# Mixture-of-experts kernel: gates read in eleven pieces at first, 40 instead of 32 first halves computed ahead

## The chip, the cores and the metric
One core of a Trainium2 chip runs the whole program. The metric is the device time of one execution in microseconds. Lower is better.

## What is computed
The reference runs two blocks on 512 tokens of width 1024. The first block has a convolution and a recurrent mixer, then sparse attention. The second block has a short convolution with pooling, then a layer of 16,384 small experts, then a gated projection. Only the expert layer is touched here:

```
q = (xb @ w_q).reshape(T, PEER_HEADS, 2, PEER_HALF)
s = jnp.einsum('thpd,hpkd->thpk', q, sub_keys)
sv, si = lax.top_k(s, PEER_TOPK)
...
gate = jax.nn.softmax(top_s.astype(jnp.float32), axis=-1).astype(xb.dtype)
u = jnp.take(expert_u, eidx, axis=0)
act = jax.nn.gelu(jnp.einsum('thkd,td->thk', u, xb))
v = jnp.take(expert_v, eidx, axis=0)
return jnp.einsum('thk,thkd->td', gate * act, v)
```

Each token chooses 16 experts for each of 8 heads. The experts lie in a grid of 128 by 128 keys.

## The kernel before
**Two ways to apply the experts.** 352 of the tokens (`TD`) go the dense way. All 16,384 experts are applied to them, and a matrix of gates that is mostly zero picks the chosen ones. The other 160 tokens go the gathered way: 160 row reads from `ue` and 160 from `ev`, 512 KB each, are fetched by indices. The reads are issued by GpSimd (line 1338), and VectorE multiplies them (lines 1353 and 1369).

**The dense way.** The code calls a row of 128 of the grid's experts one expert `e`, so there are 128 of them. The first half of an expert is `u_phase`: 24 matmuls over 352 columns give `x` times its weights `uT`, and ScalarE takes the gelu (line 1199). Weights come as four loads of 128 KB (line 201). ScalarE makes a rounded copy `wh` (line 207), and GpSimd makes the rest `wl` (line 209). The second half multiplies the result by the gates (line 1234), splits it into two parts `wwh` and `wwl` (lines 241 and 242), loads the weights `ev[e]` of 512 KB (`vraw`, line 1241), splits those too, and does 24 matmuls over 352 columns (lines 1264 to 1266). `prep` prepares three experts at a time (`GV`), one group ahead of the matmuls.

**Gates.** `route` finds the chosen experts on VectorE. Then it builds the dense gates by one-hot matrices (lines 1519 to 1536). Eleven groups of 32 tokens leave for a DRAM tensor `gs` by eleven stores (line 1537). In the expert loop `g4` brings the gates back, for four experts at a time: 704 KB, issued on ScalarE's queue (line 1227). The inner run of such a read is 512 B.

**First halves ahead.** While `route` runs, `ahead` computes the first halves of `NS` experts. The list `early` holds all `e` that 4 divides, and with more than 32 of them next 1, 9, 17 and so on. A result goes to the DRAM tensor `ga` (line 1208, 176 KB), and is read back in the loop (line 1230). After each of them `pull(GE)` lets on average `GE` of the 320 row reads go. In the expert loop `pull(GR)` does so for each expert.

**Memory.** The pools of `route` (`rp`, `rk`) and the pool `wx` are closed before the loop's pool `vp` opens. `vp` takes their addresses. `wx` holds `wrawx`, an extra seventh buffer of the `uT` weights, which are used in turn: six are `wraw`, the seventh is `wrawx`. In the address map of the kernel before, the first `g4` buffer begins where `wrawx` lies, and `vraw` lies over the one-hot tiles.

**Order.** The order of instructions on each engine is fixed at build time. The class `Order` makes several plans with a cost model of its own and `impose` writes the shortest plan into the program. In it, the first use of every tile of `vp` waits for all members of the pools that lie under `vp`, and later writes of the same tile follow the first. For DMAs from SP and ScalarE it counts eight transfers in flight:

```
if len(lanes) >= self.LANES:
    t = max(t, lanes[-self.LANES] + 900)
```

An instruction that waits holds up everything behind it on its engine. ScalarE's DMA issues stand in the same queue as its copies and gelus.

Of the kernel before, what the change touches and what calls it, by code (L numbers as in the profile page):

```python
# [133 lines left out]
class Net:  # L134
# [1038 lines left out]


    UQ = 1
    NS = 32
    GV = 3
    GA = 4
    BW = 6
# [2 lines left out]
    def peer(self):  # L1182
        nc, tc, I = self.nc, self.tc, self.I
        self.pair.close()
        self.psum2 = None
        with ExitStack() as L:
# [4 lines left out]
            gs = dr.tile([self.TD // 32, 128, 128, 32], F32, name="gs")  # L1191
            ga = dr.tile([self.NS, 128, self.TD], F32, name="ga")
            self.gather_open(L)
            up = L.enter_context(tc.tile_pool(name="up", bufs=1))

            def u_phase(e, keep):
                ps = self.proj(I["uT"][e], xh, xl)
                g = up.tile([128, self.TD], F32, name="ga", bufs=self.GA) if keep else ps
                nc.scalar.activation(g, ps, AF.Gelu_apprx_tanh)  # L1199
                return g  # L1200

            with ExitStack() as RT:
                self.wx, self.wxn = RT.enter_context(tc.tile_pool(name="wx", bufs=1)), self.PX
                early = sorted(range(128), key=lambda e: (e % 4 + 4 * (e // 4 % 2) * (e % 4 == 1), e))[:self.NS]

                def ahead():
                    for i, e in enumerate(early):
                        nc.scalar.dma_start(ga[i], u_phase(e, True))
                        self.pull(self.GE)
                        yield  # L1210
# [5 lines left out]
            with ExitStack() as VP:  # L1216
                vp = VP.enter_context(tc.tile_pool(name="vp", bufs=1))
                g4 = None
                GV = self.GV

                def prep(e0):
                    nonlocal g4
                    wh, wl, vh, vl = [], [], [], []
                    for e in range(e0, min(128, e0 + GV)):
                        if e % 4 == 0:
                            g4 = vp.tile([128, self.TD // 32, 4, 32], F32, name="g4", bufs=2)
                            nc.scalar.dma_start(g4, gs[:, :, e:e + 4, :].rearrange("g k e t -> k g e t"))
                        if e in early:
                            g = up.tile([128, self.TD], F32, name="ga", bufs=self.GA)
                            nc.scalar.dma_start(g, ga[early.index(e)])  # L1230
                        else:
                            g = u_phase(e, False)
                        gv = g.rearrange("p (g t) -> p g t", t=32)
                        nc.vector.tensor_tensor(gv, gv, g4[:, :, e % 4, :], OP.mult)
                        h = vp.tile([128, self.TD], F32R, name="wwh", bufs=self.BW)
                        l = vp.tile([128, self.TD], F32R, name="wwl", bufs=self.BW)
                        self.split(h, l, g)
                        wh.append(h)
                        wl.append(l)
                        raw = vp.tile([128, 1024], F32, name="vraw", bufs=2)  # L1240
                        nc.sync.dma_start(raw, I["ev"][e])
                        h = vp.tile([128, 1024], F32R, name="vh", bufs=self.BV)
                        l = vp.tile([128, 1024], F32R, name="vl", bufs=self.BV)
                        nc.scalar.activation(h, raw, AF.Copy)  # L1244
                        if e % 8 in self.VD:
                            nc.vector.tensor_tensor(l, raw, h.bitcast(F32), OP.subtract)
                        else:
                            nc.gpsimd.tensor_tensor(l, raw, h.bitcast(F32), OP.subtract)  # L1248
                            self.pool = self.last()
                        self.pull(self.GR)  # L1250
                        vh.append(h)
                        vl.append(l)
                    return wh, wl, vh, vl

                nxt = prep(0)
                for e0 in range(0, 128, GV):
                    wh, wl, vh, vl = nxt
                    if e0 + GV < 128:
                        nxt = prep(e0 + GV)
                    for m in range(8):  # L1260
                        po = self.bank(("xu", "tp", "xu", "nb")[m % 4])[:, 0:self.TD]
                        s = slice(128 * m, 128 * m + 128)
                        for i in range(len(wh)):
                            nc.tensor.matmul(po, vh[i][:, s], wh[i], start=(i == 0), stop=False)  # L1264
                            nc.tensor.matmul(po, vh[i][:, s], wl[i], start=False, stop=False)  # L1265
                            nc.tensor.matmul(po, vl[i][:, s], wh[i], start=False, stop=(i == len(wh) - 1))  # L1266
                        xm = self.x[m][:, 0:self.TD]
                        nc.vector.tensor_tensor(xm, po, xm, OP.add)  # L1268
                self.pull(999)
                self.gather_close()  # L1270
# [4 lines left out]
    TB = 32  # L1275
    VD = (1, 5)
    GN = 5
    GE = 2.0
    GR = 2.0

    def gather_open(self, L):
# [631 lines left out]
```

## Time and profile before

| | us |
|---|---|
| median of 3 runs | 2848.27 |
| lowest and highest | 2845.97, 2852.17 |
| the profiled execution | 2844.42 |
| its span in the profile | 2842.7 |

The profiled execution has 1.7 us around its span. Times in the profile count from the start of the span. The route ends with the last store of gates near 1807 us, and the expert loop's first second-half matmul is at 1872.85 us. PE is TensorE, DVE is VectorE, ACT is ScalarE, POOL is GpSimd; a `q` behind a name is that engine's DMA issue queue.

### The profile page before, as it was taken

Reading aid. Unit: us, or ns where it says so; the run is one execution under the profiler, and the core shown is the slowest. Engines: PE = TensorE matmul, PEld = TensorE weight load, DVE = VectorE, ACT = ScalarE, POOL = GpSimd, SP = SyncE. Lnnn points to the kernel's source line nnn. Section 1 sums busy time; section 2 is a strip of 40 time slices with the busy share of each in tenths; the row PEclk is TensorE's granted clock in tenths of the full one; section 3 lists DMA queues with packets and bytes.
Section 4 is the critical chain, followed back from the end, with each engine's and each line's share of the span. In section 5 each row is a group of like instructions: output and inputs, shape, how many; then the busy total and the mean of one; then the engine's idle time right before and its main releaser. Section 6 shows DMA issues by size and latency. Waiting matters only on the chain. (4 is left out here: it accounts for less than half of the span.)

```text
span 2842.7 us, 45654 instructions
## 1 busy us (share of the span) xinstructions
PE 2609.6 (92%) x14715; PEld 2220.0 (78%) x14715; DVE 2154.0 (76%) x4307; ACT 1481.2 (52%) x3177; POOL 1724.6 (61%) x1870
## 2 busy tenths in 40 slices
PE   5889999999798899999999987779999999999996
PEld 3656667666576688887888777779999999999995
DVE  6686669865379998954669999667877787787875
ACT  6646557568455358965353367424334333344435
POOL 4423523222164443346657788779988888899973
PEclk9889899999899999999999999989999999999998
DMA  8744355555872221223334356889999999999972
GB/s 260 172 96 97 82 117 119 103 145 122 216 241 91 71 80 46 71 84 106 92 111 141 107 193 251 293 299 326 338 321 334 334 337 335 309 334 330 336 253 80
DMA packets 353444, 552.27 MB, mean 194 GB/s; under 512 B 60082, under 2 KB 239154, under 8 KB 351539
## 3 DMA queue, kind: packets, MB, share of 16 engines
q1 hardware_dynamic: 224690, 295.22, 32.2%
q0 software_dynamic: 64800, 201.88, 23.9%
q10 hardware_dynamic: 63712, 52.24, 5.8%
q8 instruction: 116, 1.90, 0.3%
q14 instruction: 126, 1.02, 0.1%
HBM read 507.76 MB, written 41.42 MB: 193 GB/s over the span
## 5 line engine op out<-in xcount | busy, mean ns | idle before, releaser
L209 POOL TENSOR_TENSOR wl<-wraw,wh 128x256 fp32r<-128x256 f32 x937 | 748.3, 816 | 395.8 <-ACT wh L207 314.8
L207 ACT ACTIVATE wh<-wraw 128x256 fp32r<-128x256 f32 x937 | 363.0, 411 | 422.0 <-PE mm L217 198.2
L216 PE MATMUL mm<-xh,wh 128*128 128x352 f32 (+1 forms) x1464 | 513.2, 352 | 32.4 <-ACT wh L207 17.4
L218 PE MATMUL mm<-xh,wl 128*128 128x352 f32 (+1 forms) x1464 | 510.6, 352 | 18.8 <-POOL wl L209 18.8
L217 PE MATMUL mm<-xl,wh 128*128 128x352 f32 (+1 forms) x1464 | 510.5, 350 | 2.3 <-DVE xl L287 2.3
L216 PEld LDWEIGHTS mm<-xh,wh 128*128 128x128 f32 x1464 | 280.5, 192 | 57.2 <-ACT wh L207 21.0
L218 PEld LDWEIGHTS mm<-xh,wl 128*128 128x128 f32 x1464 | 280.5, 192 | 42.1 <-POOL wl L209 24.5
L217 PEld LDWEIGHTS mm<-xl,wh 128*128 128x128 f32 x1464 | 280.8, 192 | 23.3 <-DVE xl L287 4.6
L192 POOL DMA_DIRECT2D dl<-in_wev x114 | 100.7, 904 | 284.1 <-ACT dl L191 261.3
L1248 POOL TENSOR_TENSOR vl<-vraw,vh 128x1024 fp32r<-128x1024 f32 x96 | 230.9, 2407 | 4.0 <-ACT vh L1244 3.0
L1369 DVE SCALAR_TENSOR_TENSOR wide<-grow,gdot,wide 128x1024 f32<-128x1024 f32 x158 | 202.4, 1281 | 17.1 <-DMA grow<-in_ev,gidx 15.9
L218 PE MATMUL mm<-xh,dl 128*128 128x512 f32 x456 | 197.0, 436 | 15.5 <-DMA dl<-in_wev 15.5
L1353 DVE SCALAR_TENSOR_TENSOR gscr<-grow,wide 128x1024 bf16<-128x1024 f32 x160 | 194.1, 1213 | 19.4 <-DMA grow<-in_ue,gidx 18.1
L1199 ACT ACTIVATE mm<-mm 128x352 f32<-128x352 f32 x96 | 43.0, 448 | 314.4 <-PE mm L218 308.5
L216 PE MATMUL mm<-xh,dh 128*128 128x512 f32 x456 | 193.4, 428 | 13.0 <-ACT xh L355 12.3
L1338 POOL DMA_INDIRECT grow<-in_ue,gidx x160 | 164.2, 1026 | 57.8 <-DVE gscr L1353 20.2
L217 PE MATMUL mm<-xl,dh 128*128 128x512 f32 x456 | 191.1, 422 | 6.2 <-DVE xl L356 6.2
L1338 POOL DMA_INDIRECT grow<-in_ev,gidx x160 | 162.6, 1016 | 42.8 <-issue 18.1
L1244 ACT ACTIVATE vh<-vraw 128x1024 fp32r<-128x1024 f32 x128 | 134.4, 1054 | 83.2 <-DMA vraw<-in_ev 70.5
L1264 PE MATMUL xu<-wwh,vh 128*128 128x352 f32 x512 | 167.0, 326 | 5.2 <-DVE x L1268 2.6
L1266 PE MATMUL xu<-wwh,vl 128*128 128x352 f32 x512 | 166.1, 326 | 4.6 <-POOL vl L1248 2.6
L1265 PE MATMUL xu<-wwl,vh 128*128 128x352 f32 x512 | 165.8, 324 | 0.0
(582 smaller groups left out, 6818.7 us busy)
## 6 DMA issues: line engine op xcount, KB each, us to landing
vraw<-in_ev SPq DMA_DIRECT2D x128, 512.0 KB, 5.7
wraw<-in_uT SPq DMA_DIRECT2D x494, 128.0 KB, 4.7
draw<-in_wev SPq DMA_DIRECT2D x114, 256.0 KB, 3.4
dl<-in_wev POOLq DMA_DIRECT2D x114, 256.0 KB, 4.7
gs<-st SPq DMA_DIRECT2D x11, 2048.0 KB, 7.7
g<-gs ACTq DMA_DIRECT2D x32, 704.0 KB, 10.3
wraw<-in_wod SPq DMA_DIRECT2D x156, 128.0 KB, 2.2
adaw<-in_adaT SPq DMA_DIRECT2D x32, 512.0 KB, 8.1
```

The lines of the kernel that those rows point to most:

```text
L207: nc.scalar.activation(wh, raw[:, s], AF.Copy)
L209: nc.gpsimd.tensor_tensor(wl, raw[:, s], wh.bitcast(F32), OP.subtract)
L216: nc.tensor.matmul(ps, wh, xh, start=start, stop=False)
L217: nc.tensor.matmul(ps, wh, xl, start=False, stop=False)
L218: nc.tensor.matmul(ps, wl, xh, start=False, stop=stop)
L1248: nc.gpsimd.tensor_tensor(l, raw, h.bitcast(F32), OP.subtract)
L1264: nc.tensor.matmul(po, vh[i][:, s], wh[i], start=(i == 0), stop=False)
L1265: nc.tensor.matmul(po, vh[i][:, s], wl[i], start=False, stop=False)
L1266: nc.tensor.matmul(po, vl[i][:, s], wh[i], start=False, stop=(i == len(wh) - 1))
L1338: self.nc.gpsimd.indirect_dma_start(out=t, out_offset=None, in_=src, in_offset=bass.IndirectOffsetOnAxis(ap=self.gidx[i][:, k:k + 1], axis=0))
L1353: nc.vector.scalar_tensor_tensor(scr, u, 1.0, x, op0=OP.mult, op1=OP.mult, accum_out=self.gdot[i][:, k:k + 1])
L1369: nc.vector.scalar_tensor_tensor(acc, r, w, acc, op0=OP.mult, op1=OP.add)
```

## The change
`NS` becomes 40 and `GE` becomes 1.6. So eight more first halves (of experts 1, 9, 17, 25, 33, 41, 49 and 57) are computed ahead, and the number of row reads released in that stage stays 64. The first two reads of gates, for experts 0 to 3 and 4 to 7, become eleven DMAs each, one for each group of 32 tokens, 64 KB apiece.

```
-    NS = 32
+    NS = 40
...
                         if e % 4 == 0:
                             g4 = vp.tile([128, self.TD // 32, 4, 32], F32, name="g4", bufs=2)
-                            nc.scalar.dma_start(g4, gs[:, :, e:e + 4, :].rearrange("g k e t -> k g e t"))
+
+                            for i in range(self.TD // 32 if e < 8 else 0):
+                                nc.scalar.dma_start(g4[:, i], gs[i, :, e:e + 4, :])
+                            if e >= 8:
+                                nc.scalar.dma_start(g4, gs[:, :, e:e + 4, :].rearrange("g k e t -> k g e t"))
...
-    GE = 2.0
+    GE = 1.6
```

## Rows read from the trace of the kernel before

**Rows 1.** The page: busy time of each engine.
```profile
PE 2609.6 (92%) x14715; PEld 2220.0 (78%) x14715; DVE 2154.0 (76%) x4307; ACT 1481.2 (52%) x3177; POOL 1724.6 (61%) x1870
```

**Rows 2.** Stages: length, busy time and count per engine, granted clock, DMA share, rate.
```profile
core 0: us, PE busy (x) PEld busy (x) DVE busy (x) ACT busy (x) POOL busy (x), PEclk, DMA share, GB/s
...
1640.00:1807.00 167.00, 133.69 (x943) 122.93 (x942) 163.70 (x183) 123.08 (x322) 136.12 (x105) 0.97 0.61 222
1807.00:1836.00 29.00, 23.21 (x121) 21.54 (x120) 14.20 (x24) 8.22 (x21) 20.50 (x26) 0.87 0.96 354
1836.00:1858.00 22.00, 8.01 (x39) 7.36 (x38) 3.70 (x8) 2.32 (x7) 8.48 (x11) 0.66 0.94 318
1858.00:1873.00 15.00, 9.69 (x36) 8.17 (x37) 10.86 (x16) 5.69 (x14) 12.34 (x12) 0.72 0.81 267
1873.00:2340.00 467.00, 454.29 (x2755) 447.73 (x2754) 356.78 (x596) 178.60 (x390) 414.20 (x399) 0.99 0.95 329
2340.00:2760.00 420.00, 416.52 (x2572) 414.59 (x2571) 328.83 (x434) 170.76 (x353) 376.99 (x359) 1.00 0.94 322
2600.00:2700.00 100.00, 100.00 (x622) 100.00 (x621) 81.71 (x107) 41.01 (x86) 93.03 (x89) 1.00 0.97 336
```

**Rows 3.** Stages again, line 1199 alone: the gelu that ends a first half.
```profile
core 0: us, ACT busy (x), PEclk, DMA share, GB/s
...
1640.00:1807.00 167.00, 5.38 (x10) 0.97 0.61 222
1807.00:1847.00 40.00, 3.04 (x7) 0.86 0.98 346
```

**Rows 4.** Stages again, line 1338 alone: the row reads on POOL.
```profile
core 0: us, POOL busy (x), PEclk, DMA share, GB/s
...
1807.00:1847.00 40.00, 13.01 (x15) 0.86 0.98 346
...
1873.00:2340.00 467.00, 149.63 (x150) 0.99 0.95 329
```

**Rows 5.** Route's last stage (1640 to 1807), PE by line: busy, mean ns, idle before.
```profile
L1533 PE MATMUL tp<-o,o 128*128 128x128 f32 x352 | 49.9, 283 | 14.8 <-ACT st L1536 6.6 <-DVE o L1519 5.5 <-ACT wh L207 2.0
L1533 PE MATMUL xu<-o,o 128*128 128x128 f32 x352 | 49.8, 280 | 12.8 <-POOL o L1528 12.8
```

**Rows 6.** Timeline at the start of the expert loop: start, length, engine, instruction, wait.
```profile
1834.86 0.74 POOL L209 TENSOR_TENSOR wl<-wrawx,wh 128x256 fp32r<-128x256 f32 x1
...
1835.63 0.80 SPq L1241 DMA_DIRECT2D vraw<-in_ev  x2
1835.63 0.43 ACTq L1227 DMA_DIRECT2D g<-gs  x1
...
1836.16 5.23 ACTq L1227 DMA_DIRECT2D g<-gs  x1
...
1857.25 0.34 ACTq L1230 DMA_DIRECT2D ga<-ga  x1
1857.64 0.42 ACT L207 ACTIVATE wh<-wraw 128x256 fp32r<-128x256 f32 x1 [10.50 <-DMA g<-gs]
...
1858.11 0.66 PE L216 MATMUL mm<-xh,wh 128*128 128x352 f32 x1 [14.10 <-ACT wh L207]
```

**Rows 7.** PE's timeline: the first matmul of a second half.
```profile
1872.85 0.35 PE L1264 MATMUL xu<-wwh,vh 128*128 128x352 f32 x1
```

**Rows 8.** The chain that ended last, in order of time: the first read of gates.
```profile
1836.16 21.08 DMA g<-gs
```

**Rows 9.** The DMAs of the loop's first half (1873 to 2340).
```profile
DMA packets 84935, 153.85 MB, mean 329 GB/s; under 512 B 7152, under 2 KB 57440, under 8 KB 84891
...
wraw<-in_uT SPq DMA_DIRECT2D x199, 128.0 KB, 4.9
g<-gs ACTq DMA_DIRECT2D x17, 704.0 KB, 10.6
```

**Rows 10.** The tile g: issues, nanoseconds min/median/max.
```profile
L1227 ACTq DMA_DIRECT2D g<-gs x32: 377/377/5231, 1835.6 to 2694.2; - x32
```

**Rows 11.** DMAs from 1800 to 1880: KB each, median us to landing.
```profile
ga<-ga ACTq DMA_DIRECT2D x12, 176.0 KB, 5.4
g<-gs ACTq DMA_DIRECT2D x2, 704.0 KB, 16.7
```

## The prediction
> **What bounds the kernel now.** I read the page first, then the stages, then the timeline where they change. TensorE is busy 92% of the span [rows 1], but what limits it differs by stage.
>
> In the last stage of the route (1640 to 1807) VectorE is busy 163.7 of 167 us and TensorE 133.7 [rows 2]. So VectorE sets the pace there, and TensorE has 33 us free. It waits there for the makers of the one-hot tiles [rows 5]. The DMA engines are at 0.61.
>
> From 1807 on only first halves are left to compute before the loop can open. Seven of them end between 1807 and 1847 [rows 3], together with 15 row reads [rows 4]. The DMA share is 0.98 at 346 GB/s [rows 3], so this stage is bound by DMA and not by TensorE.
>
> Then comes a hole. The loop's pool opens when the last reader of `wrawx` ends at 1834.86 + 0.74 = 1835.60; both the first read of gates and the first `vraw` are issued at 1835.63 [rows 6]. That read takes 21.08 us [rows 8]. ScalarE's next-but-few DMA, the read of `ga` at line 1230, is issued only at 1857.25, and the copy behind it shows 10.50 us of waiting for `g<-gs`; TensorE has by then waited 14.10 us [rows 6]. The first second-half matmul is at 1872.85 [rows 7], 37.2 us after the pool opened, and TensorE issued only 39 + 36 = 75 matmuls in it [rows 2].
>
> The loop's first half (1873 to 2340) has TensorE at 454 of 467 us and DMA at 0.95. The second half has TensorE at 417 of 420, DMA at 0.94 [rows 2]. Both resources are nearly full, so work moved from one to the other hardly pays. At full pace a 352-column matmul takes 100/622 = 0.161 us [rows 2], so a first half costs TensorE 24 x 0.161 = 3.86 us.
>
> **The change part by part.**
>
> *Eight more first halves ahead.* In the route they could use free TensorE time. But seven first halves were already left over at 1807, so the plan had more than enough of them and still placed none of the seven in the route. I therefore take that none of the eight fits there; the bound on the other side is all 33 us of free time, some eight of them. So at the end of the route 15 are left instead of 7. The 7 took 40 us: 40 x 346/1000 = 13.8 MB, of which 15 rows are 7.9 MB. A first half needs 4 x 128 KB of weights and a 176 KB write, 0.70 MB together [rows 9, 11]. With 1.6 rows of 0.524 MB it is 1.54 MB, or 4.5 us at 346 GB/s, above TensorE's 3.86. For 15 that is 67 us, so this stage grows by **27 us** (by TensorE alone 15 x 3.86 - 40 = 18; at the old 40/7 = 5.7 us each 46). About 24 rows go in it, 9 more than the 15 before.
>
> *The loop without them.* All eight belong to its first half (experts 1 to 57). TensorE loses 8 x 3.86 = 31 us of work. DMA loses 8 x 0.524 = 4.2 MB of weights, gains 8 x 0.18 = 1.4 MB of reads of `ga`, and loses the 9 rows that went earlier, 4.7 MB. That leaves 153.85 - 7.5 = 146.4 MB [rows 9], at 329 GB/s 445 us for 467: **-22 us**. The bounds are -31 (TensorE alone) and -8 (DMA without the moved rows). ScalarE's and GpSimd's copies for the weights move too: 4 x 8 on each, GpSimd being at 414 of 467 us in the first half [rows 2], so it only gains room there. The second half of the loop stays as it is.
>
> *The pieces.* They don't start earlier by themselves: the first piece's buffer still waits for the pools beneath it, and the other ten follow the first, while all stores of gates were issued by 1807. What they change is how long one transfer is in flight. ScalarE's read of `ga` waited for the 704 KB read to end, though it needs nothing of it; I read this as the limit of eight transfers in flight, which the plan's own code has. A 64 KB piece frees its place sooner. The first reads of both kinds moved 1.4 MB in about 21 us [rows 8, 11]. If this goes on at the same rate, the first eleven pieces are in after some 11 us and the reads of `ga` some 7 us later (the 176 KB ones took 5.4 [rows 11]). With the multiplication and the split, some 3 us, the first second half starts near 22 us after the opening, for 37 now.
>
> The cost is on ScalarE: 20 more issues of 0.377 us [rows 10] are 7.5 us, and what is queued behind them are the weight copies that TensorE waits for. ScalarE is busy only 8.0 of 37 us in this stretch [rows 2], so I count them as hidden; uncovered they are +7.5. Also `wrawx` comes round every seventh weight tile. Before, 36 of the 39 matmuls after the opening were cover, six tiles behind the last `wrawx`. Eight first halves are 32 tiles, and 6 + 32 leaves 3 after it by the turn of seven. So 18 matmuls of cover remain, 2.9 us less. Work done in the hole: before 75 x 0.161 = 12 us in 37; after, 18 + 48 (two first halves, as many as the banks hold) = 66, or 10.6 us in 22. The loss falls from 25 to 11. I take **-12 us**, with bounds -17 (an opening of 19 us) and +3 (no quicker landing, less cover), +10 with the issues uncovered.
>
> The Trainium skill (DMA: Bandwidth & Descriptors, "Measured (HBM→SBUF, 128 partitions, SWDGE, issued from GpSimd)") speaks against the pieces: it says to batch transfers to 1 MiB or more, and that 64 KB reaches a third of the rate. By its table a 64 KB transfer is 0.95 us, so an estimate from that page is 10.5 us for eleven in a row, where one of 704 KB would be near 4.4 (between its rows of 64 KB and 1 MB); with 6 us more for the first read the sum below would be -1. No run here has a 64 KB read yet; the 21.08 us of the whole read [rows 8] is far above either, since it shared the engines with row reads.
>
> **Sum.** +27 - 22 - 12 = -7 us on the profiled 2844.4, giving 2837. The profiled execution lies 3.9 us under the median of the runs, so I forecast **2841** for the median. Clearly told from no change is about 0.2%, 5.7 us.
>
> **Rivals.**
>
> *The route takes some of the eight* (chance 0.17). Then they cost nothing twice: TensorE had 33 us free, DMA 39% free [rows 2]. Each one placed takes 4.5 us off the stage after 1807, but its 1.6 rows, 2.5 us of DMA, fall back on the loop: 2 to 4.5 us, say 3. Four to eight of them give -7 - 12 to -7 - 24: 2817 to 2829. For it: 40 candidates give the plan more choice. Against: seven left over at 1807 [rows 3].
>
> *The pieces don't help* (0.25): no faster, or slower. The same bytes on the same queue behind the same row reads; ScalarE still stands until the last piece of the second read has a place. Then the hole gives +3, and the sum is 27 - 22 + 3 = +8: 2856, from 2850 to 2860. The Trainium skill (DMA: Bandwidth & Descriptors, "Queues, rings and completion order") speaks for this rival: by it each DMA engine takes turns between the queues that have work, and this doesn't depend on how one queue's work is cut. For it: the long landing [rows 8]. Against: the wait of 10.50 us was on a place and not on data [rows 6].
>
> *The pieces hurt* (0.12): slower. 22 of them take places from the weight loads on SP, 8 at a time; 22 / 8 is nearly three rounds, at the 5.4 us that a 176 KB transfer took [rows 11] 15 us in which SP's loads get few places. Together with 7.5 us of issue it decides from the point where both reads of gates are placed before the reads of `ga`. The hole then grows by about 10 and the sum is +15: 2863.
>
> *As forecast* (0.44): -7, its own range -15 to 0, which reaches into no change. The rest, 0.02, is a plan that falls out otherwise, to either side.
>
> **How the numbers follow.** Faster by over 0.2%: 0.27 of the forecast's 0.44, all of the first rival's 0.17, and 0.01 of the rest: 0.45. Within 0.2%: 0.17 of the forecast and 0.10 of the second rival: 0.27. Slower: 0.15 of the second rival, 0.12 of the third, 0.01: 0.28. The range from 2820 to 2860 takes in the forecast, the second rival and most of the first; it leaves out the third and the deepest gains.
>
> **What the profile after would show.** About 15 gelus of line 1199 between the last store of gates and the loop, at some 4.5 us each; fewer means that the route took them. The first second-half matmul some 22 us behind the last `wrawx` reader; 37 or more refutes the pieces' part. ScalarE's wait on `g<-gs` under 5 us. Some 20 us less between the first second half and expert 64, with DMA still near 0.95 there; if it falls to 0.9, I have the wrong bound and the gain goes to 31. The last 400 us unchanged. The prediction is wrong if the plan moves the route itself, whose end at 1807 I hold fixed.

## The result, and the profile after

The changed kernel takes 2871.71 us (median of 12 runs, 2850.67 to 2884.69). The kernel before took 2847.28 us beside it (12 runs, 2838.88 to 2858.21). The ratio is 1.0079, 95% interval [1.0054, 1.0104], so the change costs 22 to 24 us. The forecast was 2841, a gain of 7, with a range up to 2860. It was wrong in sign and in range.

The profiled execution of the changed kernel took 2884.69 us, the highest of its 12, so part of its difference is chance. The tile `ga` shows how much. Below is its first row for three executions, in this order: the kernel before, the changed kernel, and the changed kernel once more (experiment e3). The last columns are the first and last issue in us.

```profile
L1208 ACTq DMA_DIRECT2D ga<-ga x32: 326/326/2201, 1483.2 to 1858.9; - x32
```
```profile
L1208 ACTq DMA_DIRECT2D ga<-ga x40: 326/327/361, 1501.5 to 1943.1; - x40
```
```profile
L1208 ACTq DMA_DIRECT2D ga<-ga x40: 326/326/365, 1486.8 to 1929.2; - x40
```

The first result of a first half is written 18.3 us later in the changed kernel, but only 3.6 us later in its second profile. Up to about 1420 us the instructions stand in the same order in both kernels. So the 18 us belong to that execution, and I compare stages by their lengths. A view of stages does this. First comes the kernel before, cut at the last store of gates, at the opening of the loop's pool, at the first second-half matmul, and after 21 of the loop's 43 groups of experts. (The cuts differ a little from those of [rows 2].)

```profile
core 0: us, PE busy (x) PEld busy (x) DVE busy (x) ACT busy (x) POOL busy (x), PEclk, DMA share, GB/s
1806.90:1835.60 28.70, 22.97 (x120) 21.30 (x118) 13.90 (x23) 8.22 (x21) 20.20 (x26) 0.88 0.96 355
1835.60:1872.90 37.30, 17.93 (x75) 15.77 (x76) 14.86 (x23) 7.91 (x19) 21.12 (x24) 0.68 0.89 297
1872.90:2323.90 451.00, 438.29 (x2655) 431.73 (x2655) 343.12 (x580) 173.54 (x378) 399.45 (x385) 0.99 0.95 329
2323.90:2765.60 441.70, 438.05 (x2715) 435.81 (x2713) 345.06 (x456) 176.37 (x365) 391.85 (x373) 1.00 0.93 319
```

The same four stages of the changed kernel, same columns:

```profile
1824.50:1895.20 70.70, 56.15 (x298) 52.66 (x297) 36.08 (x61) 22.20 (x62) 58.55 (x74) 0.92 0.99 354
1895.20:1927.10 31.90, 17.50 (x71) 14.92 (x69) 20.23 (x32) 8.74 (x16) 26.10 (x26) 0.77 1.03 380
1927.10:2351.00 423.90, 409.20 (x2496) 403.46 (x2497) 334.19 (x541) 169.85 (x347) 362.66 (x342) 0.99 0.94 325
2351.00:2804.60 453.60, 437.99 (x2673) 432.97 (x2672) 348.07 (x449) 175.78 (x354) 387.07 (x359) 0.99 0.89 303
```

Ahead of the opening the changed kernel takes 42.0 us more (70.7 for 28.7), with 178 more matmuls. From the opening to the first second half it takes 5.4 us less. The loop's first part takes 27.1 less and its second part 11.9 more, though the second part has about the same work (2673 matmuls for 2715). In all that is +42.0 - 5.4 - 27.1 + 11.9 = +21.4 us. In the second profile of the same kernel the terms are +43.9, -5.8, -16.2 and +8.1, together +30.0. These two sums bracket the 24.4 us between the medians.

The row reads (line 1342 here) explain part of the first stage. It issues 29 of them, where the 28.7 us stage of before had 11 (the same view of line 1338; [rows 4] counts 15 up to 1847):

```profile
1824.50:1895.20 70.70, 27.54 (x29) 0.92 0.99 354
```

The waits on gates moved from ScalarE to VectorE. ScalarE's one wait of 10.50 us [rows 6] is now at most 2.1. The views of waits (total us, times, longest) show it, first ScalarE from 1895 to 1930, then VectorE in the loop:

```profile
ACT wh L207 <- DMA g<-gs: 5.8, 4, 2.1
```
```profile
DVE ga L1238 <- DMA g<-gs: 39.1, 11, 6.8
```

In the loop of before VectorE's wait for gates was 1.8 us, two times.

### The profile page after: what moved, and what is told of

Read it like the earlier page. It is cut to its first block, busy times and chain, and to the rows that moved or that the text cites. A ratio compares the mean times of both kernels' runs of the same rounds, so it can differ in the third digit from the quotient of the medians.

```text
span 2882.8 us, 45750 instructions
## 1 busy us (share of the span) xinstructions
PE 2630.4 (91%) x14715; PEld 2229.8 (77%) x14715; DVE 2176.1 (75%) x4307; ACT 1493.7 (52%) x3177; POOL 1727.1 (60%) x1870
## 3 DMA queue, kind: packets, MB, share of 16 engines
q1 hardware_dynamic: 224690, 295.22, 31.9%
## 5 line engine op out<-in xcount | busy, mean ns | idle before, releaser
L207 ACT ACTIVATE wh<-wraw 128x256 fp32r<-128x256 f32 x932 | 370.2, 413 | 577.3 <-PE mm L217 329.7
L216 PE MATMUL mm<-xh,wh 128*128 128x352 f32 (+1 forms) x1464 | 513.8, 353 | 31.3 <-ACT wh L207 12.6
L216 PEld LDWEIGHTS mm<-xh,wh 128*128 128x128 f32 x1464 | 280.9, 192 | 55.6 <-ACT wh L207 15.2
L1342 POOL DMA_INDIRECT grow<-in_ue,gidx x160 | 160.5, 1003 | 48.4 <-issue 18.2
L1342 POOL DMA_INDIRECT grow<-in_ev,gidx x160 | 161.5, 1009 | 41.7 <-issue 16.2
L790 DVE SCALAR_TENSOR_TENSOR x<-u,vec,x 128x512 f32<-128x512 f32 x184 | 145.5, 791 | 13.8 <-ACT x L788 11.4
```

What stands on the lines that cost most here:

```text
L207: nc.scalar.activation(wh, raw[:, s], AF.Copy)
L216: nc.tensor.matmul(ps, wh, xh, start=start, stop=False)
L1342: self.nc.gpsimd.indirect_dma_start(out=t, out_offset=None, in_=src, in_offset=bass.IndirectOffsetOnAxis(ap=self.gidx[i][:, k:k + 1], axis=0))
```

## The experiments

Eighteen more runs were made, each beside the kernel before on the same chip. For each the table gives the ratio to the kernel before and three lengths in us from one profile each. "Opening" runs from the last store of gates to the first second-half matmul. "Loop" runs from there to the last addition to `x` (line 1268, or 1272 with the pieces). "Layer" runs from the first gelu of a first half to the same end, so it leaves out everything upstream. "Ahead" is `NS`, the first halves computed ahead. "Weight" is a constant of the planner's rule for the order (`alpha`). It decides which of the ready instructions goes first, and both kernels had chosen 100.

| run | ahead | reads | `GE`, `GR` | weight | ratio | opening | loop | layer |
|---|---|---|---|---|---|---|---|---|
| before | 32 | whole | 2.0, 2.0 | 100 | 1 | 66.0 | 892.7 | 1282.9 |
| after | 40 | pieces | 1.6, 2.0 | 100 | 1.0079 | 102.6 | 877.5 | 1303.6 |
| e1 | 32 | pieces | 2.0, 2.0 | 100 | 1.0011 | 55.4 | 908.5 | 1290.0 |
| e2 | 40 | whole | 1.6, 2.0 | 100 | 1.0050 | 99.3 | 872.3 | 1301.7 |
| e3 | 40 | pieces | 1.6, 2.0 | 100 | 1.0087 | 104.1 | 884.6 | 1313.2 |
| e4 | 40 | pieces | 0.8, 2.25 | 100 | 1.0051 | 79.5 | 885.9 | 1290.0 |
| e5 | 32 | whole | 2.0, 2.0 | 105 | 1.0007 | 57.8 | 899.0 | 1287.7 |
| e6 | 40 | pieces | 1.6, 2.0 | 105 | 1.0075 | 107.1 | 888.0 | 1317.0 |
| e7 | 32 | whole | 2.0, 2.0 | 120 | 1.0079 | 33.5 | 922.1 | 1304.7 |
| e8 | 40 | pieces | 1.6, 2.0 | 120 | 0.9972 | 39.7 | 896.0 | 1305.4 |
| e9 | 32 | whole | 1.0, 2.25 | 100 | 0.9995 | 50.7 | 910.9 | 1287.6 |
| e10 | 32 | pieces | 1.0, 2.25 | 100 | 0.9945 | 51.9 | 886.1 | 1263.0 |
| e11 | 32 | whole | 1.9, 2.0 | 100 | 1.0030 | 72.3 | 886.9 | 1285.7 |
| e12 | 40 | whole | 0.8, 2.25 | 100 | 1.0115 | 72.5 | 909.2 | 1306.2 |
| e13 | 40 | pieces, 3 buffers | 1.6, 2.0 | 100 | 1.0085 | 112.1 | 878.4 | 1310.0 |
| e14 | 32 | whole, 3 buffers | 2.0, 2.0 | 100 | 0.9999 | 61.3 | 890.9 | 1282.8 |
| e15 | 32 | pieces, 3 buffers | 1.0, 2.25 | 100 | 1.0057 | 53.8 | 923.3 | 1297.2 |
| e16 | 40 | pieces, 3 buffers | 0.8, 2.25 | 100 | 1.0050 | 76.3 | 894.2 | 1297.1 |
| e17 | 24 | pieces | 1.33, 2.25 | 100 | 0.9989 | 33.1 | 925.0 | 1280.6 |
| e18 | 32 | pieces | 1.0, 2.25 | 105 | 0.9990 | 40.7 | 905.6 | 1275.8 |

**Each part alone, and the whole again (e1 to e3).** e1 is the pieces alone:

```
-                            nc.scalar.dma_start(g4, gs[:, :, e:e + 4, :].rearrange("g k e t -> k g e t"))
+                            for i in range(self.TD // 32 if e < 8 else 0):
+                                nc.scalar.dma_start(g4[:, i], gs[i, :, e:e + 4, :])
+                            if e >= 8:
+                                nc.scalar.dma_start(g4, gs[:, :, e:e + 4, :].rearrange("g k e t -> k g e t"))
```

> Only the eleven pieces; 32 first halves and 2 row reads each as before. If the eight more first halves cost the time, this run is within 6 us of before (ratio 0.998 to 1.002), and the first second half starts some 55 to 62 us after the last store of gates instead of 66, as the pieces end the wait of ScalarE. If the pieces cost it, the ratio is 1.005 or more and the opening is later than 66 us after the last store. If a new order of the whole loop costs it, the loop after its first group is longer or shorter by 5 us or more although it holds the same work.

Measured: 1.0011 [0.9988, 1.0033]. Its stages, opening and loop:

```profile
1805.20:1860.60 55.40, 40.15 (x196) 36.78 (x195) 30.32 (x50) 18.18 (x43) 44.92 (x50) 0.85 1.02 377
1860.60:2769.10 908.50, 880.88 (x5359) 872.50 (x5359) 721.13 (x1032) 350.23 (x740) 794.30 (x755) 0.98 0.94 319
```

The opening is 10.6 us shorter than before and the loop 15.8 longer, with the same number of matmuls (5359 for 5370). Of the 10.6 us, 6.4 lie ahead of the pool's opening (22.3 us for 28.7), where no piece has been issued, and 4.2 behind it:

```profile
1805.20:1827.50 22.30, 19.13 (x107) 18.53 (x107) 11.90 (x20) 7.16 (x18) 15.84 (x20) 0.92 1.00 375
1827.50:1860.60 33.10, 21.01 (x91) 18.25 (x89) 18.42 (x30) 11.02 (x25) 29.09 (x31) 0.80 1.04 378
```

The opening of e5 below, the work of before in another order and with whole reads, is as short (57.8 us). So this pair does not show that the pieces shorten it, and the time does not move.

e2 is the forty alone:

```
-    NS = 32
+    NS = 40
...
-    GE = 2.0
+    GE = 1.6
```

> Only 40 first halves and 1.6 row reads each; the first two reads of gates whole as before. If the eight more cost the time, the ratio is near the whole change's 1.008 (1.005 to 1.011), with some 100 us between the last store of gates and the first second half. If the pieces cost it, the ratio is near 1.000. If the pieces helped as I forecast, by 12 us, this run is slower than the whole change: 1.012.

Measured: 1.0050 [1.0025, 1.0075]. Opening 99.3 us, loop 872.3: +33.3 and -20.4. The opening ahead of and behind the opening of the pool:

```profile
1815.90:1889.50 73.60, 60.12 (x302) 54.99 (x301) 37.08 (x61) 22.75 (x63) 60.24 (x77) 0.87 0.97 345
1889.50:1915.20 25.70, 14.79 (x69) 12.63 (x69) 12.49 (x20) 7.38 (x17) 19.01 (x21) 0.77 1.05 365
```

The second line is the hole of the prediction. With whole reads it is shorter here (25.7 us) than with the pieces (31.9 in the changed kernel), and none of ScalarE's waits in it is put down to `g<-gs`.

e3 is the changed kernel with nothing edited.

> The changed kernel unaltered, for a second profile of the same order of instructions. If the order is what lost 18 us in the loop's second half, that loss (half of the groups to the last group: 440 us for 422) is there again within 3 us. If it was a chance of one execution, it is gone. The 18 us that were lost before the experts began, where the instructions are the same as before, are chance by every theory and should come out at another size.

Measured: 1.0087 [1.0054, 1.0119], so the loss repeats. The larger part of the cost lies with the forty.

**Fewer row reads ahead (e4, e9, e10, e12).** In e4 half as many reads go with the first halves, and the loop gets them back:

```
-    GE = 1.6
-    GR = 2.0
+    GE = 0.8
+    GR = 2.25
```

> The whole change, but the row reads released ahead go from 64 to 32 (GE 0.8), and the loop's from 2 to 2.25 for each expert, so that the sum is 320 again. If row reads crowd out the weights ahead of the loop, the 75 us between the last store and the last first half ahead fall to 55 or less, and the loop gets longer by what these reads cost there, 32 x 0.524 MB at 329 GB/s or 51 us at most; the total is then the same within 6 us of the whole change if DMA is the bound everywhere, and lower by 10 or more if TensorE has room in the loop. If the plan's order decides and not the bytes, the total moves by 10 us or more to either side and the stage ahead does not follow the rows.

Measured: 1.0051 [1.0027, 1.0075]. Its stage ahead of the opening, and the row reads in it:

```profile
1817.40:1867.90 50.50, 49.41 (x294) 47.46 (x294) 15.37 (x25) 24.05 (x62) 43.41 (x59) 1.00 0.90 307
```
```profile
1817.40:1867.90 50.50, 9.39 (x10) 1.00 0.90 307
```

The changed kernel needed 70.7 us for 298 matmuls here. e4 needs 50.5 us for 294, with 10 row reads in place of 29. At 0.161 us each 294 matmuls are 47.3 us, and the granted clock is full, so TensorE now bounds the stage. In the changed kernel the row reads did: 19 x 0.524 MB at 354 GB/s is 28 us of DMA, and 20 us of it showed. Some of the 20 may be the clock's, 0.92 in the one and 1.00 in the other. From the store to the last gelu of these first halves e4 took 61.3 us, where the expectation for crowding rows was 55 or less.

e9, e10 and e12 do the same to the kernel before, to e1 and to e2. The edit of e9 and e10, and behind it that of e12 against e2:

```
-    GE = 2.0
-    GR = 2.0
+    GE = 1.0
+    GR = 2.25
```
```
-    GE = 1.6
-    GR = 2.0
+    GE = 0.8
+    GR = 2.25
```

> The kernel before with 32 row reads released ahead instead of 64 and 2.25 instead of 2 for each expert in the loop (320 in all). If row reads cost their full DMA time ahead of the loop and little in it, the way from the last store of gates to the first second half falls from 66 us to 45 to 58, and the loop grows by less than 10 us for some 10 more rows: total 0.1 to 0.5% below before. If the loop is bound by DMA, as I forecast, it grows by 10 x 1.6 = 16 us and the total is the same or higher.

> As the run before, with the eleven pieces for the first two reads. If the pieces end the stall at the opening whatever else is there, the way from the store to the first second half is 8 to 12 us shorter than in the run before. If that gain was one order's, it is within 3 us or longer.

> 40 first halves with 32 row reads released ahead and 2.25 in the loop, the gates read whole: the fourth run without the pieces. If the pieces cost nothing and help little among 15 leftover first halves, this equals that run within 0.2% (1.005). If the rows are what the eight more cost, it lies below 40 first halves with 64 rows (1.005) by 0.2% or more, and its opening is 15 us or more shorter than that run's 99.4 us.

Measured: 0.9995 [0.9974, 1.0016], 0.9945 [0.9924, 0.9967] and 1.0115 [1.0084, 1.0147]. e10 beats both kernels. Its opening is 51.9 us, 1.2 longer than that of e9 with whole reads, so what the pieces gained in e1 was that order's. e12's stage ahead of the opening shrinks as e4's did, with 7 row reads where e2 had 29 in 73.6 us:

```profile
1808.40:1857.30 48.90, 48.90 (x301) 48.90 (x300) 10.68 (x17) 23.72 (x63) 40.72 (x56) 1.00 0.89 285
```

But e12's loop is 909.2 us for 872.3 in e2, and the time rises where the expectation had it fall. The stages of e10:

```profile
1818.10:1870.00 51.90, 37.70 (x198) 36.24 (x196) 26.57 (x44) 18.91 (x46) 41.56 (x48) 0.85 1.00 360
1870.00:2756.10 886.10, 873.91 (x5359) 863.41 (x5359) 699.26 (x1042) 350.85 (x738) 795.92 (x760) 1.00 0.95 331
```

This loop moves 331 GB/s and is 6.6 us shorter than that of before, at 324 GB/s over the same stretch. So DMA alone does not set the loop's time. One pair does not settle it: e9, with the same edit, has a loop 18.2 us longer than before, as a loop bound by DMA would.

Five pairs at weight 100 differ in `NS` and keep all else and `GE` x `NS` equal. In before and e2, e1 and e3, e9 and e12, e10 and e4 the ratio rises from 32 to 40 by 0.50, 0.76, 1.20 and 1.06 points. In the fifth, e15 and e16 (below), it falls by 0.07.

**How much does an order matter by itself? (e11, e5 to e8).** e11 moves three row reads in 320:

```
-    GE = 2.0
+    GE = 1.9
```

> The kernel before with 1.9 for 2.0 row reads released with each first half ahead: some three of 320 rows later, no other edit; the plan is made anew. The bytes and the work are those of before, so by any theory of bytes or matmuls the total is within 0.1%, the loop 893 us within 5 and TensorE's loss in it 30 within 5. If a newly drawn order costs the loop 10 to 20 us by itself, as I suspect of the pieces alone (loop 908.5 us for 892.7), the loss is 40 to 50 here too and the total 0.3 to 0.6% higher.

Measured: 1.0030 [1.0010, 1.0050], for next to no change of work. The loop of its profile is 5.8 us shorter, not 10 to 20 longer, and its opening 6.3 longer. e5 and e6 are the kernel before and the changed one with weight 105, e7 and e8 the same two with 120 in the place of 105:

```
-    nc = build(A, Order(build(A)).best()[1])
+    nc = build(A, Order(build(A)).best((105,))[1])
```

> The work of before, unchanged, in another plan (the one parameter of the plan's priorities is 105 where the kernel before picked 100). If a new order of the loop is worth 10 to 20 us by itself, this run differs from before by 0.3% or more, and TensorE's loss in the loop, 30 us in before (time less matmuls x 0.161), comes out at 40 to 55. If orders of the same work are alike, it is within 0.2% and the loss within 5 us of 30.

> The changed kernel in the same other plan, 105. If the eight first halves ahead cost time by themselves, it is slower than the run before it by 0.4% or more, as with 100. If the loss came from the order that the change happened to draw, the two are within 0.3% of each other, or the other way round.

> The work of before in a third plan, 120. As for the plan 105: by the theory of the order it lies 0.3% or more from at least one of the other two plans of the same work; by the other theory all three are within 0.2%.

> The changed kernel in the third plan, 120. If its work costs the time, it is slower than the run before it by 0.4% or more here too, with 30 us or more added between the last store of gates and the first second half, and less than that taken from the loop. If the order decides, the sign changes among the three pairs.

Measured: 1.0007 [0.9989, 1.0025] and 1.0075 [1.0048, 1.0101] at 105; 1.0079 [1.0047, 1.0112] and 0.9972 [0.9951, 0.9994] at 120. At 105 the change costs what it did at 100. At 120 the sign turns. The layer does not account for it, since it takes 1304.7 us with 32 ahead and 1305.4 with 40. The difference lies ahead of it, where the first gelu comes at 1483.5 and at 1466.7 us: 16.8 of the 19.6 us between the two spans. These orders differ upstream too, so the ratios of this pair say little of the change. Its layers say that eight more ahead cost 0.7 us here, for 29.3 at 105. Nearly all first halves go into the route in these orders (1 and 3 are left at the last store), and the route is longer for it: 349.2 and 369.8 us from the first gelu to the last store of gates, for 324.2 in the kernel before with 7 left. The pair does show that one program in three orders spreads over 0.8% (before, e5, e7).

**Late gates in the loop? (e13 to e16).** The theory: the loop gives back too little since VectorE waits some 40 us for reads of gates. A third buffer lets each read start a turn earlier:

```
-                            g4 = vp.tile([128, self.TD // 32, 4, 32], F32, name="g4", bufs=2)
+                            g4 = vp.tile([128, self.TD // 32, 4, 32], F32, name="g4", bufs=3)
```

e13 is the changed kernel with it, e14 the kernel before, e15 is e10 and e16 is e4. In e14 and e16 the weight is held to 100 as well, which the kernels without the edit had.

> The changed kernel with three buffers instead of two for the reads of gates, nothing else. Theory of late gates: VectorE's idle time ended by the gates' transfer falls from 39 to 43 us in the loop to under 10, the loop shortens by 15 to 20 us from some 880, and the time comes to 0.999 to 1.003 of the kernel before. Rival, the drawn order: those waits may fall, but TensorE's lost time in the loop stays at 45 to 55 us and the time stays at 1.005 to 1.011.

> The kernel before with three buffers for the reads of gates, its planner held to the weight that it took before. Theory of late gates: there are only 1.8 us of such waits to remove, so the time stays within 0.2% of before. Rival, the drawn order: a new order of the loop alone may move it by 0.3% or more in either direction.

> The fastest version so far (32 first halves, pieces, fewer row reads ahead; 0.9945) with the third buffer. It shows 5.8 us of waits for gates in the loop, so by the theory of late gates it gains at most 6 us: 0.9925 to 0.9945. By the drawn order it may lose its lead: 0.994 to 1.002.

> Forty first halves, pieces, fewer row reads ahead (1.0051 with two buffers) with the third buffer, the planner held to the same weight. With two buffers it waits 10.9 us for gates in the loop but loses 56 us of TensorE there. Theory of late gates: it gains at most 11 us, 1.001 to 1.004. Rival: TensorE's loss does not follow those waits, and the time stays at 1.003 to 1.008 or moves by a draw.

Measured: e13 1.0085 [1.0064, 1.0106], e14 0.9999 [0.9989, 1.0010], e15 1.0057 [1.0037, 1.0078], e16 1.0050 [1.0027, 1.0072]. VectorE's waits for gates in the loop, in e3 and then in e13:

```profile
DVE ga L1238 <- DMA g<-gs: 42.8, 11, 7.4
```
```profile
DVE ga L1238 <- DMA g<-gs: 19.8, 4, 7.2
```

The waits halve, 23 us less, and the ratio stays. Nor do the waits follow the time elsewhere. e16 and then e4 have as many of them and the same ratio:

```profile
DVE ga L1238 <- DMA g<-gs: 11.4, 5, 4.0
```
```profile
DVE ga L1238 <- DMA g<-gs: 10.9, 6, 4.8
```

e15 has 9.9 us, 4 more than e10, and its loop is 37 us longer:

```profile
1861.00:2784.30 923.30, 884.73 (x5358) 868.06 (x5358) 730.11 (x1048) 346.25 (x741) 805.86 (x763) 0.99 0.93 319
```

The theory falls: these waits end VectorE's idle time and mostly not TensorE's.

**Fewer than 32, and the lead of e10 (e17, e18).** The edit of e17 against e10, and behind it that of e18 against e10:

```
-    NS = 32
-    GE = 1.0
+    NS = 24
+    GE = 1.33
```
```
-    nc = build(A, Order(build(A)).best()[1])
+    nc = build(A, Order(build(A)).best((105,))[1])
```

In e17 the weight was fixed at 100, as e10 has it.

> 24 experts' first halves ahead instead of 32, in pieces, with as many row reads ahead as in the version at 0.9945 (32 over the halves), the planner's weight the same. Theory that each eight past what fits beside the route costs 0.5 to 1.2%: with 24 none is left after the last store of gates, the time from that store to the first matmul of the second halves falls from 52 us to 30 to 40, the loop takes back eight first halves (31 us of TensorE) and lengthens by 25 to 32 us: 0.992 to 0.998. Rival: TensorE stands idle in the opening with nothing to do, the loop pays all 31 us, and the time comes to 0.999 to 1.006.

> The version at 0.9945 with the planner's weight at 105 instead of 100, so the same instructions in another order. If its lead belongs to the design (a shorter opening, fewer reads in it): 0.992 to 0.998. If it belongs to the order that it drew: anywhere from 0.994 to 1.006, most likely above 0.998.

Measured: e17 0.9989 [0.9967, 1.0012], e18 0.9990 [0.9971, 1.0010]. The stages of e17:

```profile
1811.50:1844.60 33.10, 2.46 (x17) 2.16 (x15) 19.41 (x34) 4.50 (x9) 20.98 (x21) 0.58 1.02 373
1844.60:2769.60 925.00, 907.45 (x5552) 899.04 (x5552) 728.78 (x1054) 365.21 (x776) 822.34 (x789) 0.99 0.94 321
```

With no first half left over the opening still takes 33.1 us, and TensorE does 17 matmuls in it. The loop takes 38.9 us more than in e10. The theory's 30 to 40 us for the opening held, the loop's 25 to 32 did not: TensorE stood in the opening and the loop paid in full, as the rival said. The ratio lies at the rival's edge. In e10's opening 198 matmuls, 32 us of work, cost 18.8 us over e17's. In e4's 390 matmuls cost 27.6 us over e10's, for 31 us of work. In these orders the first seven left over are partly free; the next eight are paid nearly in full.

e18 shows that e10's lead is mostly that of the order it drew. e10 remains the fastest version that ran, but its design is at best a few tenths of a per cent ahead of the kernel before.

## Why the prediction was wrong

**The stage ahead of the opening, forecast +27.** Of the eight only one went into the route, near the none that I took it to be. 14 were left over at the last store of gates (forecast 15, before 7), and the route kept its length: 323.5 us from the first gelu to that store for 324.2. The stage was bound by DMA, also as said. The step that failed is "With 1.6 rows of 0.524 MB it is 1.54 MB, or 4.5 us". It took the mean of row reads per first half for the number in this stage. By the prediction's own cut, from the last store to the last gelu, the stage took 75.9 us for 40.3, with 32 row reads where I counted about 24:

```profile
1824.50:1900.40 75.90, 29.93 (x32) 0.91 0.99 355
```

These are 32 / 14 = 2.3 rows for each first half. With 0.70 MB of its own that is 1.90 MB, or 5.4 us at 355 GB/s, and 14 of them took 5.4 us each. That is near the 5.7 of before, which I held only as the bound (46). The reason stands in the route. Up to the last store of gates 24 row reads are issued in either kernel, before and then after, so most of the 64 that go with the first halves are left for what follows:

```profile
1400.00:1806.90 406.90, 28.47 (x24) 0.98 0.48 161
```
```profile
1400.00:1824.50 424.50, 27.38 (x24) 0.98 0.48 161
```

By the prediction's cut the term measured +35.6. By the cut at the pool's opening it is +42.0 and +43.9 (e3), since the opening now comes 4.7 us ahead of the last gelu and came 11.1 ahead before. e4 and e12 show the cause by taking the rows away: 20 and 25 us less in this stage.

**The hole after the opening, forecast -12.** It measured -5.4, -5.8 and -4.2: the first second half comes 31.9, 31.5 and 33.1 us after the opening (after, e3, e1) for 37.3, not 22. That the pieces did even this is not shown. ScalarE stood 10.50 us before, which the prediction read as the wait for a place. With whole reads it stands behind a DMA issue for 5.7 us at most in e2 and 7.2 in e9, neither put down to the gates, and their holes are 25.7 and 29.7 us. So a good part of that stand, and all of the hole's gain, can come from the order alone. The 22 pieces are issued over 39 us, the first at 1896.2 and the last at 1935.1, with ScalarE's copies between them in the planned order:

```profile
L1229 ACTq DMA_DIRECT2D g<-gs x22: 326/327/1867, 1896.2 to 1935.1; - x22
```

The eleventh is issued at 1911.84, 16.6 us after the opening, so "the first eleven pieces are in after some 11 us" failed. Nor did the first second half of the changed kernel wait for them. From issue to landing the pieces took 10.2 us at most, so the eleventh was in by 1922.4. VectorE took up the first gates at 1926.02, right behind multiplications for row reads, five of which had waited 6.5 us in sum for their rows. The first of the five and the gates:

```profile
1915.26 1.22 DVE L1357 SCALAR_TENSOR_TENSOR gscr<-grow,wide 128x1024 bf16<-128x1024 f32 x1 [1.81 <-DMA grow<-in_ue,gidx]
...
1926.02 0.52 DVE L1238 TENSOR_TENSOR ga<-ga,g 128x352 f32<-128x352 f32 x1
```

The rival that the pieces do not help was nearer in the total (e1, 1.0011), and these runs do not refute it.

The Trainium skill (DMA: Bandwidth & Descriptors, "Measured (HBM→SBUF, 128 partitions, SWDGE, issued from GpSimd)") holds that transfers be batched to 1 MiB and that 64 KB reaches a third of the rate. No run here tests that for these reads by themselves. The hole moved 380 GB/s at a DMA share of 1.03 with the pieces and 297 at 0.89 with the whole reads of before, but 365 at 1.05 with the whole reads of e2. So these rates follow what the other queues do, and not the size of the reads.

**The loop, forecast -22.** It measured -15.2 (after) and -8.1 (e3). Two steps failed. One is "The second half of the loop stays as it is": the first part gave back 27.1 and 16.2 us, about what was forecast for it, and the second lost 11.9 and 8.1. The other is the price by bytes, "at 329 GB/s 445 us for 467". The whole loop moved 275.5 MB for 289.2 (877.5 us at 314 GB/s for 892.7 at 324). These 13.7 MB less are 42 us by that price. The DMA share fell to 0.89 in the second part, and the gain of 31 that the prediction tied to such a fall did not come. TensorE is the fuller engine in the loop, but not at its full pace. 5370 matmuls at 0.161 are 864.6 us of 892.7 before; 5169 are 832.2 us of 877.5 after. 32.4 us of work left, and TensorE's loss rose from 28 to 45 us. Waits that the profile shows make up most of that: TensorE's idle time in the loop (length less busy time) is 16.4 us before, 30.3 after and 34.4 in e3. The largest of them in e3 is a wait for VectorE's addition to `x`:

```profile
PE xu L1268 <- DVE x L1272: 10.9, 8, 3.7
```

In the kernel before the same wait was 2.6 us, and in e13, with half the waits for gates, it was 12.9:

```profile
PE xu L1264 <- DVE x L1268: 2.6, 4, 1.4
```
```profile
PE xu L1268 <- DVE x L1272: 12.9, 8, 4.2
```

This VectorE work stayed in the loop while TensorE's went. But the wait does not follow the forty: e1, with 32 ahead, has more of it than e3, and e2, with 40, has 5.3 us.

```profile
PE xu L1268 <- DVE x L1272: 13.7, 8, 5.2
```

So it is not shown to be what the forty cost.

**Over all orders.** One profile of one order is a poor witness here: loops with 32 ahead and the same matmuls ran 886 to 923 us. I therefore average over the profiles with weights 100 and 105. Nine with 32 ahead (before, e1, e5, e9, e10, e11, e14, e15, e18) have an opening of 56.7 and a loop of 900.4 us, and a mean ratio of 1.0004. Eight with 40 (after, e2, e3, e4, e6, e12, e13, e16, where e3 is after once more) have 94.2, 886.3 and 1.0074. So eight more ahead cost 37.5 us in the opening and give back 14.1 in the loop. From the spread within each set (12.6 and 11.5 us) the 14.1 has a standard error of some 6 us, so the 31 that TensorE gave up came back only in part. From pair to pair the loop gave back between 0.2 us (e10 and e4) and 31.0 (e1 and after). The layer is 1283.6 and 1304.9 us, +21, which is the measured loss within its error. With the two programs at weight 120 the picture is the same: openings of 54.3 and 88.1, loops of 902.6 and 887.3, ratios of 1.0011 and 1.0063.

The same averages (100 and 105) price the row reads. With half of them ahead the opening falls from 62.6 to 49.3 us with 32 ahead and from 105.0 to 76.1 with 40. The loop grows from 895.6 to 906.5 and from 880.2 to 896.4. So rows taken out of the opening come back in the loop in part.

**Rivals.** "The route takes some" was refuted: one of the eight went there. Nor would they have been free, if the orders at weight 120 are a guide (six more in the route than before, and 25 us more of it, in e7). "The pieces hurt" was the case that came nearest to the time, 2863, but by a mechanism that did not act. SP's weight loads waited no longer for places behind gates. Its waits from the opening to the first second half, in the kernel before and in e1:

```profile
SPq L201 <- DMA g<-gs: 8.9, 1, 8.9
```
```profile
SPq L201 <- DMA g<-gs: 7.9, 7, 2.1
```

The true case, that the moved work is paid ahead and returned only in part, was not among the rivals. I had it as the bounds 46 and -8 of two terms and did not put them together: 46 - 8 - 12 = +26. That this comes near the measured time is partly luck, as the -12 was about -5.

**Open.** Why the loop does not return the 31 us is not settled. Late gates are not the price as far as e13 shows, which halved them. Left are VectorE's share of the loop and the orders that the planner draws; these were not separated.

## What to carry to other kernels

Work moved ahead of a stage pays only as far as it fills idle time there: count what is left over when the cover ends, price each at the old stage's own rate per item (here 5.7 us, not the 4.5 worked out from a mean), and don't credit the later stage with the full time that it loses. Where an order of instructions is planned at build time, build the same work under two or three orders before believing half a per cent; here three row reads more or less moved the time by 0.3%, and a gain of 10.6 us in one stage was lost in the next. A stage that gets shorter in one order is no proof either: the hole shrank as much with the reads left whole. A wait that ends an engine's idle time is not a price until it is removed and the time falls.

## What the runs showed of the hardware

- TensorE's granted clock rose in the middle of busy work. In the changed kernel's opening it was 0.50, the lower of its levels (1.2 of 2.4 GHz), from 1895.4 to 1897.1 and 1.00 from 1897.6 on, with TensorE busy throughout. The two stretches, and two matmuls of them from the timeline:

```profile
1895.40:1897.10 1.70, 1.70 (x7) 1.70 (x7) 1.67 (x3) 0.42 (x1) 1.70 (x3) 0.50 0.99 399
1897.60:1899.10 1.50, 1.50 (x12) 1.50 (x11) 1.40 (x3) 0.00 (x0) 1.20 (x2) 1.00 0.93 323
```
```profile
1896.59 0.49 PE L217 MATMUL mm<-xl,wh 128*128 128x352 f32 x1
...
1897.61 0.32 PE L218 MATMUL mm<-xh,wl 128*128 128x352 f32 x1
```

  The mean over an opening went with how much TensorE stood in it: 0.58 in e17's (17 matmuls in 33.1 us), 0.85 in e10's (198 in 51.9), 0.94 in e4's (390 in 79.5). So part of the loss in an opening can be the clock's.
- 64 KB pieces took a median of 6.0 us to land in e1 (1820 to 1860) at 377 GB/s in all, hardly less than the 7.1 us of the 128 KB weight loads beside them. Half the size made little difference with the engines this full.
- The same instructions reached the expert layer 18.3 us later in one execution of the changed kernel than in one of the kernel before, and 3.6 us later in another. A difference of this size between two profiles need not be the change's.
